# Two plain pairs and one pair ahead at the start of each projection, their results kept until the blocks are made

## The chip, the cores and the metric

The kernel runs on one core of one Trainium2 chip. The metric is the device time of one execution in microseconds (us). Its engines have queues of their own: TensorE (PE) multiplies, VectorE (DVE) and ScalarE (ACT) do elementwise work, GpSimd (POOL) issues transfers here, SyncE (SP) issues most transfers. PEld is TensorE's loading of weights.

## What is computed

Two layers of a hybrid encoder trunk over 1024 tokens of width 1024. Cut to what matters:

```python
for l in range(DEPTH):                      # DEPTH = 2
    h = rmsnorm(x, norm1_w[l])
    q, k, v, g, z, xbc, dt_raw, lru_gate, lru_x = split_proj(h @ w_in[l])
    y_ret = retention(q, k, v, g)
    y_ssd = ssd(z, xbc, dt_raw, ...)
    y_lru = rglru(lru_gate, lru_x, ...)
    y = jnp.concatenate([y_ret, y_ssd, y_lru], axis=-1)
    x = x + (y @ w_out[l]).astype(x.dtype)
    h = rmsnorm(x, norm2_w[l])
    x = x + conv_ffn(h, ffn_w_up[l], ffn_conv_w[l], ffn_conv_b[l], ffn_w_down[l])
return rmsnorm(x, final_norm_w)
```

`conv_ffn` multiplies by `ffn_w_up`, runs a causal convolution of width 3 over the tokens, gates one half with the other and multiplies by `ffn_w_down` (2816 wide). The ssd part runs a convolution of width 4 over x, B and C, and takes its step sizes dt from eight columns of the projection through a softplus; their running sums (cum) make the decays.

## The kernel before

**Products.** Everything is float32. A number is split into a high part of type fp32r and a low rest, and each product takes three passes: high times high, high times low, low times high. The high part of a weight is a ScalarE copy (L236), the low part a VectorE subtraction (L243) or, in the steady state (`by_dma`), a second ScalarE copy and a transfer that POOL issues and that subtracts on the way (L241). An operand's low part is L206. A `product` here is 12 matmuls of 128x512: four slices of the contraction, three passes each.

**Four projections.** Each layer has two: the input projection (12 pairs of 128-column weight tiles, in an order written out by hand) and the feed-forward up projection (22 pairs). Each pair meets the 1024 tokens in two halves of 512, and the width of 1024 in two halves, so a pair is a 2 by 2 block product. In the plain way that takes 8 products. By the Winograd form of Strassen's scheme it takes 7, with sums of weight tiles (`prep`, L710: named wr and s) and sums of operand blocks. The operand blocks have names: b11 and b21 are the first token half, made early from a normalised half (XA); t1, b22, t2, t3 and t4 need the second half (XB) and its norm too, and `blocks_b` makes them in this order: XB is scaled by its norm `rows` (L744, L746, L750), then differences (L710) and splits (L206).

**The opening of a projection.** `products` starts with `lead` pairs in the plain way and `ahead` pairs begun in the Winograd way, before the second half's norm and blocks are there. `lead` makes the first token half of a plain pair from b11 and b21 (4 products; the second of two added at L809), `follow` the second half from t1 and b22 (4 products, L822). `start` makes the first token half of a Winograd pair (2 products, L837), `end` the other 5, with t2, t3, t1, b22 and t4 in that order (L874 to L890). Between the leads `rest(j)` does the steps of the second half's norm and blocks. Before the change lead is 1 and ahead 2 everywhere:

```python
        n = lead + ahead
        for j, p in enumerate(pairs[:n]):
            if j < lead:
                p.lead(raw)
            else:
                p.start(True, raw)
            if j < n - 1:
                rest(j)
        rest(2)
```

**What is done with a result.** Each finished tile goes to the pair's `take` at once: in the feed-forward part the convolution (`conv`: a ScalarE step L315 and VectorE steps L318, tile fc) and the gate (L933); in the input projection a rotation for q and k (L382 to L384, tiles c, u, qs, tb), a convolution for x, B and C (L318 and L393, tile xb), gelu, silu or the LRU's gates. In layer 0 the first leads run on unnormalised input and are multiplied by the norm `raw` afterwards (L847, L848).

**dt and cum.** `steps` multiplies dt's 16 columns (L403, 16 matmuls for one half of the tokens, tile dt, summed to dtc at L407 to L415), transposes the result on TensorE (L418, bank dtt), and adds the bias (L421, L422). `ssd_dt` runs the softplus on VectorE in small steps (L173 to L182), multiplies to da, makes running sums with two small matmuls (L506, L507, tile cum), and transposes the sums (L519). Each engine has its own list of instructions, in the order in which the program was built.

## Time and profile before

| | |
|---|---|
| median of three runs | 2349.01 us (2347.21 to 2349.03) |
| the profiled execution | 2346.2 us |
| its span | 2344.4 us |
| PE, DVE, ACT busy share of the span | 93%, 82%, 55% |
| granted TensorE clock, mean | 0.97 of full speed |

The span is the time from the first to the last instruction of the profiled execution; 1.8 us lie around it. An engine is busy while it works on an instruction; what it waits for is shown by the idle time ahead of an instruction and by what released it. In a timeline an operation's duration is longer than the time to the next one's start, since neighbours overlap by some 0.08 us.

### The profile page before, as it was taken

The numbers are of one execution on the slowest core, as the hardware profiler recorded it, in microseconds if no ns is written. First come the engines' busy times: TensorE is split into PE (matmuls) and PEld (weight loads), VectorE is DVE, ScalarE is ACT, GpSimd is POOL, SyncE is SP. The second block draws the span as 40 slices with busy tenths as digits, with TensorE's granted clock in tenths as the row PEclk, the third lists the DMA queues.
The fourth block names the chain that finished last, engine by engine and source line by source line (L and its number), as shares of the span: only waits on it lengthen the run. The fifth ranks groups of instructions, "written<-read, shape, count | busy, mean of one in ns | idle before, by whom it ended". The sixth has DMA issues, their size and how long they took to land.

```text
span 2344.4 us, 31562 instructions
## 1 busy us (share of the span) xinstructions
PE 2174.7 (93%) x10494; PEld 1758.3 (75%) x10494; DVE 1924.6 (82%) x3763; ACT 1288.4 (55%) x2370; POOL 302.6 (13%) x335
## 2 busy tenths in 40 slices
PE   6699988997999999999978989899989999999997
PEld 4477767885788888878866767777668888887787
DVE  7987858779877788999798877696797788789987
ACT  5357637554566556444445674674556665654443
POOL 0012213000222222000001131210002222210000
PEclk9799999999999999999988999999989999999999
DMA  4365687561666666854334638846437666677522
GB/s 173 108 149 134 150 248 233 167 209 48 149 150 148 145 153 152 285 193 137 108 128 123 152 79 235 266 150 208 137 93 164 144 148 148 147 197 254 178 83 73
DMA packets 176147, 371.94 MB, mean 159 GB/s; under 512 B 19440, under 2 KB 31856, under 8 KB 175984
## 3 DMA queue, kind: packets, MB, share of 16 engines
q1 hardware_dynamic: 135760, 297.55, 38.6%
q0 software_dynamic: 37440, 68.17, 17.1%
q10 hardware_dynamic: 2784, 4.20, 0.5%
q8 instruction: 83, 1.36, 0.3%
q14 instruction: 80, 0.66, 0.1%
HBM read 228.22 MB, written 69.27 MB: 127 GB/s over the span
## 4 chain that ended last, share of the span: by engine, by line
PE 65%; DVE 15%; DMA 8%; issue 7%; ACT 3%; SPq 1%; POOL 1%; DVEq 0%; POOLq 0%; ACTq 0%
PE up L300 43%; PE op L300 6%; PE dy L995 5%; PE dx L995 5%; PE dx L1071 2%; DMA ws<-wr 2%; DVE ws L243 2%; DVE bl L206 1%; DVE xb L318 1%; DMA cumb<-cumscr 1%; DMA tb<-in_rope_dram 1%; DMA g<-g1scr 1%; DMA g<-g0scr 1%; DVE g L710 1%; DMA wr<-in_w_ct_dram 1%
## 5 line engine op out<-in xcount | busy, mean ns | idle before, releaser
L300 PE MATMUL up<-bh,ws 128*128 128x512 f32 x3840 | 1228.2, 400 | 76.4 <-ACT ws L236 50.5
L300 PEld LDWEIGHTS up<-bh,ws 128*128 128x128 f32 x3840 | 735.6, 192 | 249.7 <-ACT ws L236 54.0
L300 PE MATMUL up<-bl,ws 128*128 128x512 f32 x1920 | 761.1, 398 | 11.8 <-DVE bl L206 11.7
L236 ACT ACTIVATE ws<-wr 128x512 fp32r<-128x512 f32 x568 | 348.7, 626 | 358.9 <-PE up L300 129.0
L300 PEld LDWEIGHTS up<-bl,ws 128*128 128x128 f32 x1920 | 369.2, 192 | 102.3 <-DVE bl L206 22.4
L241 POOL DMA_DIRECT2D ws<-wr x222 | 197.6, 905 | 1321.5 <-ACT ws L240 1046.0
L243 DVE TENSOR_TENSOR ws<-wr,ws 128x512 fp32r<-128x512 f32 x346 | 236.5, 688 | 61.0 <-ACT ws L236 54.9
L995 PE MATMUL dy<-ws,ws 128*128 128x512 f32 x792 | 192.2, 390 | 3.2 <-ACT ws L236 1.6
L995 PE MATMUL dx<-ws,ws 128*128 128x512 f32 x792 | 190.8, 390 | 2.1 <-ACT ws L236 1.2
L995 PEld LDWEIGHTS dy<-ws,ws 128*128 128x128 f32 x792 | 148.2, 188 | 36.4 <-DVE ws L243 3.3
L995 PEld LDWEIGHTS dx<-ws,ws 128*128 128x128 f32 x792 | 148.4, 188 | 34.1 <-ACT ws L236 2.1
L318 DVE SCALAR_TENSOR_TENSOR fc<-u,smalls,fc 128x512 f32<-128x512 f32 (+2 forms) x176 | 131.0, 748 | 50.6 <-ACT fc L315 49.6
L240 ACT ACTIVATE ws<-ws 128x512 fp32r<-128x512 f32 x260 | 159.8, 626 | 4.6
L300 PE MATMUL op<-yh,ws 128*128 128x512 f32 x512 | 160.5, 394 | 0.2 <-ACT yh L213 0.2
L318 DVE SCALAR_TENSOR_TENSOR fc<-c,smalls,fc 128x512 f32<-128x512 f32 (+2 forms) x176 | 131.2, 745 | 0.7 <-ACT fc L315 0.3
L315 ACT ACTIVATE fc<-c,smalls 128x512 f32<-128x512 f32 x88 | 71.2, 809 | 103.7 <-DVE c L837 101.7
L243 DVE TENSOR_TENSOR ws<-g,ws 128x512 fp32r<-128x512 f32 (+1 forms) x165 | 103.1, 649 | 13.7 <-ACT ws L236 13.5
L236 ACT ACTIVATE ws<-g 128x512 fp32r<-128x512 f32 (+1 forms) x165 | 92.1, 590 | 39.7 <-PE dy L995 13.8
L300 PEld LDWEIGHTS op<-yh,ws 128*128 128x128 f32 x512 | 95.4, 188 | 21.7 <-ACT yh L213 2.1
L300 PE MATMUL op<-yl,ws 128*128 128x512 f32 x256 | 100.3, 394 | 0.0
L710 DVE TENSOR_TENSOR wr<-wr,wr 128x512 f32<-128x512 f32 x64 | 44.9, 702 | 63.0 <-DMA wr<-in_w_up_dram 28.3
L236 ACT ACTIVATE ws<-s 128x512 fp32r<-128x512 f32 x64 | 40.4, 632 | 101.3 <-DVE s L710 92.4
(303 smaller groups left out, 2939.3 us busy)
## 6 DMA issues: line engine op xcount, KB each, us to landing
ws<-wr POOLq DMA_DIRECT2D x222, 256.0 KB, 4.3
wr<-in_w_up_dram SPq DMA_DIRECT2D x96, 512.0 KB, 4.3
wr<-in_w_dn_dram SPq DMA_DIRECT2D x66, 512.0 KB, 3.9
wr<-in_w_ct_dram SPq DMA_DIRECT2D x56, 512.0 KB, 4.7
wr<-in_w_o_dram SPq DMA_DIRECT2D x32, 512.0 KB, 5.1
g0scr<-fc SPq DMA_DIRECT2D x44, 256.0 KB, 3.3
g<-g0scr SPq DMA_DIRECT2D x44, 256.0 KB, 5.8
g1scr<-fc SPq DMA_DIRECT2D x44, 256.0 KB, 2.9
```

What stands on the lines that cost most here:

```text
L206: eng.tensor_tensor(lo, src, hi.bitcast(F32), op=ALU.subtract)
L236: act.activation(w[:, 0, :m], raw, AF.Copy)
L240: act.activation(w[:, 1, :m], w[:, 0, :m].bitcast(F32), AF.Copy, scale=-1.0)
L241: pool.dma_start(w[:, 1, :m].bitcast(F32), raw, accum_op=ALU.add)
L243: eng.tensor_tensor(w[:, 1, :m], raw, w[:, 0, :m].bitcast(F32), op=ALU.subtract)
L300: pe.matmul(dst, W(k, a), A(k, b), start=first and i == 0, stop=last and i == n - 1)
L315: act.activation(dst, body(x), AF.Identity, bias=bias, scale=taps(n))
L318: dve.scalar_tensor_tensor(dst[:, o:HT], x[:, HALO - j + o : HALO - j + HT], taps(n - j), dst[:, o:HT], op0=ALU.mult, op1=ALU.add)
L710: eng.tensor_tensor(o, a, b, op=op)
L995: pe.matmul(d[oc], w[:, a, P * oc : P * oc + P], t[:, b], start=not more and i == 0 and k == 0, stop=i == NP - 1 and k == 2, skip_group_ch ...
L1071: pe.matmul(X[oc][:, e], w[x][:, P * oc : P * oc + P], t[:, y, e], start=False, stop=i == NP - 1 and k == 2, skip_group_check=True)
```

## The change

`products` begins with two pairs in the plain way and one in the Winograd way, in both layers and both kinds of projection. The takes of these three pairs are not called when a tile is done: `products` first runs `follow` of both plain pairs, `prep` of the pair ahead and all of `blocks_b`, then goes through the pairs and calls `firsts` (the takes of the first token half) and `followed` or `end`. t2 comes from another pool of tiles. The transposes of dt, the cum matmuls and the transposes of cum are held back by a count of products: `behind(n, f)` calls f when n more products have been issued, `tick` counts; cum's transposes get a bank of their own (cumt).

```diff
@@ -413,13 +416,17 @@
             dve.tensor_add(c, c, c1)
         else:
             dve.tensor_add(c, c1, d[0:16, :])
-        t = s_bank("dtt")
-        for i in range(4):
-            pe.transpose(t[:, 16 * i : 16 * i + 16], c[:, P * i : P * i + P], ident[0:16, 0:16])
         dt = s_tile("dt", [P, 4, 8], "dt")
-        t = t[:, 0:64].rearrange("p (c h) -> p c h", c=4)
-        dve.tensor_tensor(dt, t[:, :, 0:8], srow[:, l, 0, :].unsqueeze(1).to_broadcast([P, 4, 8]), op=ALU.add)
-        dve.tensor_add(dt, dt, t[:, :, 8:16])
+
+        def turn():
+            t = s_bank("dtt")
+            for i in range(4):
+                pe.transpose(t[:, 16 * i : 16 * i + 16], c[:, P * i : P * i + P], ident[0:16, 0:16])
+            t = t[:, 0:64].rearrange("p (c h) -> p c h", c=4)
+            dve.tensor_tensor(dt, t[:, :, 0:8], srow[:, l, 0, :].unsqueeze(1).to_broadcast([P, 4, 8]), op=ALU.add)
+            dve.tensor_add(dt, dt, t[:, :, 8:16])
+
+        behind(4, turn)
         return dt
 
     sret = {}
@@ -501,26 +508,34 @@
         softplus_of(e, dt, d, shp, "d")
         da = s_tile("da", shp, "da")
         dve.tensor_tensor(da, d, anea[:, l, :].unsqueeze(1).to_broadcast(shp), op=ALU.mult)
-        cps = s_bank("cum")
-        daf = da.rearrange("p c h -> p (c h)")
-        pe.matmul(cps[:, 0:32], tri, daf, start=True, stop=True)
-        pe.matmul(cps[:, 32:64], ones, daf, start=True, stop=True)
         cum = s_tile("cm", shp, "cm")
         ecum = s_tile("ec", shp, "ec")
         dec = s_tile("dc", shp, "dc")
         cdec = s_tile("cd", shp, "cd")
-        v = cps[:, 0:32].rearrange("p (c h) -> p c h", c=4)
-        last = cps[:, 32:64].rearrange("p (c h) -> p c h", c=4)
-        dve.tensor_copy(cum, v)
-        act.activation(ecum, cum, AF.Exp)
-        act.activation(cdec, last, AF.Exp)
-        dve.tensor_tensor(dec, last, cum, op=ALU.subtract)
-        act.activation(dec, dec, AF.Exp)
-        pe.transpose(cps[0:32, 128:256], cum.rearrange("p c h -> p (c h)"), ident)
-        ct = s_tile("ct", [32, P], "ct", 1)
-        act.activation(ct, cps[0:32, 128:256], AF.Copy)
-        sp.dma_start(scr[2 * l + h], ct)
-        dve.tensor_mul(dec, dec, d)
+
+        def sums():
+            cps = s_bank("cum")
+            daf = da.rearrange("p c h -> p (c h)")
+            pe.matmul(cps[:, 0:32], tri, daf, start=True, stop=True)
+            pe.matmul(cps[:, 32:64], ones, daf, start=True, stop=True)
+            v = cps[:, 0:32].rearrange("p (c h) -> p c h", c=4)
+            last = cps[:, 32:64].rearrange("p (c h) -> p c h", c=4)
+            dve.tensor_copy(cum, v)
+            act.activation(ecum, cum, AF.Exp)
+            act.activation(cdec, last, AF.Exp)
+            dve.tensor_tensor(dec, last, cum, op=ALU.subtract)
+            act.activation(dec, dec, AF.Exp)
+            dve.tensor_mul(dec, dec, d)
+            behind(3, turn)
+
+        def turn():
+            c = s_bank("cumt")
+            pe.transpose(c[0:32, 0:P], cum.rearrange("p c h -> p (c h)"), ident)
+            ct = s_tile("ct", [32, P], "ct", 1)
+            act.activation(ct, c[0:32, 0:P], AF.Copy)
+            sp.dma_start(scr[2 * l + h], ct)
+
+        behind(4, sums)
         return d, cum, ecum, dec, cdec
 
     def skip(l):
@@ -759,7 +774,7 @@
             put("b22", k, XB[4 + k], d_tile, d_tile)
         yield
         for k in range(4):
-            t = c_tile("t2")
+            t = t_tile("t2")
             sub(dve, t, XB[4 + k], XA[k])
             put("t2", k, t, aq_tile, aq_tile)
             scale_a(4 + k)
@@ -781,8 +796,22 @@
         sp.dma_start(r[:, : 2 * HT], src)
         return r[:, :HT], r[:, HT : 2 * HT]
 
-    def prod(d, w, B, name, first=True, last=True):
-        mm3(d, lambda k, a: w[:, a, P * k : P * k + P], lambda k, b: B[name, k][b], range(4), first, last)
+
+    pending = []
+
+    def behind(n, f):
+        pending.append([n, f])
+
+    def tick(n=1):
+        for x in list(pending):
+            x[0] -= n
+            if x[0] <= 0:
+                pending.remove(x)
+                x[1]()
+
+    def prod(d, w, B, name, first=True, last=True, more=False):
+        tick()
+        mm3(d, lambda k, a: w[:, a, P * k : P * k + P], lambda k, b: B[name, k][b], range(4), first and not more, last, more)
 
     class Pair:
@@ -790,7 +819,7 @@
         def __init__(self, src, B, take):
             self.src, self.B, self.take, self.ready, self.w, self.q = src, B, take, None, None, None
 
-        def lead(self, raw):
+        def lead(self):
 
             B = self.B
             self.v = []
@@ -808,8 +837,6 @@
                 c = halo(t_tile, "c11")
                 dve.tensor_add(body(c), body(u), d2)
                 self.v.append((c, u))
-                if not raw:
-                    self.take(m, 0, c, u)
 
         def follow(self):
@@ -820,14 +847,14 @@
                 prod(d, w1, self.B, "t1", last=False)
                 prod(d, w2, self.B, "b22", first=False)
                 dve.tensor_add(body(u), body(u), d)
+
+        def followed(self):
+            for m, (_, u) in enumerate(self.v):
                 self.take(m, 1, u)
 
-        def start(self, reload=False, raw=False):
-            if self.ready:
-                w11, w12 = self.ready
-            else:
-                q = up_raw(self.src[0])
-                w11, w12 = part_of(q[0]), part_of(q[1])
+        def start(self, reload=False):
+            q = up_raw(self.src[0])
+            w11, w12 = part_of(q[0]), part_of(q[1])
             d1, d2 = p_bank("up"), s_bank("up")
             prod(d1, w11, self.B, "b11")
             self.u = halo(c_tile, "u")
@@ -837,15 +864,17 @@
             dve.tensor_add(body(c11), body(self.u), d2)
             self.q = None if reload else q
             self.v = [(c11, self.u)]
-            if not (reload and raw):
-                self.scaled()
 
         def scaled(self):
 
-            for m, (c, u) in enumerate(self.v):
-                if "raw" in self.B:
+            if "raw" in self.B:
+                for c, u in self.v:
                     dve.tensor_tensor(body(c), body(c), self.B["raw"], op=ALU.mult)
                     dve.tensor_tensor(body(u), body(u), self.B["raw"], op=ALU.mult)
+
+        def firsts(self):
+
+            for m, (c, u) in enumerate(self.v):
                 self.take(m, 0, c, u)
 
         def prep(self):
@@ -892,31 +921,33 @@
             self.take(1, 1, C22)
 
 
-    def products(pairs, rest, later, lead, ahead, raw=False):
+    def products(pairs, rest, later, lead=2, ahead=1):
+
 
         n = lead + ahead
         for j, p in enumerate(pairs[:n]):
             if j < lead:
-                p.lead(raw)
+                p.lead()
             else:
-                p.start(True, raw)
-            if j < n - 1:
-                rest(j)
-        rest(2)
+                p.start(True)
+            rest(j)
+        for p in pairs[:lead]:
+            p.scaled()
+            p.follow()
+        pairs[lead].prep()
+        rest(3)
         for j, p in enumerate(pairs):
             by_dma[0] = j >= n
             if j >= n:
                 p.start()
-            elif raw:
+            if j >= lead:
                 p.scaled()
-            if j == 1:
-                rest(3)
-            if j < lead:
-                p.follow()
-            else:
-                p.end()
+            p.firsts()
+            (p.followed if j < lead else p.end)()
             for f in later.get(j, ()):
                 f()
+        while pending:
+            tick()
         by_dma[0] = False
 
     def ffn_pair(l, j, B):
@@ -1233,7 +1264,7 @@
             rest = lead(B, XA, XB, first[0])
             pairs[0].ready = ready
         later = {0: [] if l else [setup], 1: [dt_a, dt_b], 3: [dt_c]}
-        products(pairs, rest, later, *((1, 2) if l else (1, 2)), not l)
+        products(pairs, rest, later)
         after = mixers(l, dts, skip(l))
         XA = out_proj(l, 0, y_split(l, 0, after), src)
         SB = y_split(l, 1, last_dma[0])
@@ -1250,7 +1281,7 @@
         XB = out_proj(l, 1, SB, src, hook)
         sB = squares(lambda k: XB[k], f=d_tile)
         spill(xs1, XB, 1)
-        products([ffn_pair(l, j, B) for j in range(NF)], rest_of(B, XA, XB, sB, w2), {}, *((1, 2) if l else (1, 2)))
+        products([ffn_pair(l, j, B) for j in range(NF)], rest_of(B, XA, XB, sB, w2), {})
         XA, XB, last, others = ffn_down(l, None)
         if l + 1 < DEPTH:
             B, st = {}, {}
```

Two further hunks give `mm3` a flag that is never set and split `lru` into two functions with the same steps in the same order. Line numbers move: L809 becomes L838, L822 L849, L837 L864, L874 to L890 become L903 to L919, L710 L725, L744 L759, L933 L964, L382 to L384 become L385 to L387, L393 L396, L418 L424.

**Where instructions move.** First, VectorE in layer 0's feed-forward projection, ahead of the first Winograd pair that is not started early. Before, the sum s of the second pair ahead (s_5505) stands behind the end of the first one and among its convolution steps (fc):

```order
L886 TENSOR_TENSOR u_5123<-u_5123,up_5454 128x512
L890 TENSOR_TENSOR u_5436<-u_5436,up_5473 128x512
L710 TENSOR_TENSOR wr_5500<-wr_5500,wr_5502 128x512
L318 SCALAR_TENSOR_TENSOR fc_5468<-u_5123,smalls,fc_5468 128x512
L318 SCALAR_TENSOR_TENSOR fc_5487<-u_5436,smalls,fc_5487 128x511
L318 SCALAR_TENSOR_TENSOR fc_5468<-u_5123,smalls,fc_5468 128x512
L318 SCALAR_TENSOR_TENSOR fc_5487<-u_5436,smalls,fc_5487 128x510
L320 COPY c_5437<-u_5436 128x2
L710 TENSOR_TENSOR s_5505<-wr_5502,wr_5500 128x512
L933 TENSOR_TENSOR fc_5487<-fc_5139,fc_5487 128x512
L318 SCALAR_TENSOR_TENSOR fc_5494<-c_5437,smalls,fc_5494 128x512
L243 TENSOR_TENSOR ws_5507<-s_5505,ws_5507 128x512
```

After, the steps of all first pairs stand together ahead of the next pair's low weight part (ws_5643), and the end of the pair ahead and the sum s_5685 of the next pair follow:

```order
L318 SCALAR_TENSOR_TENSOR fc_5540<-c_5220,smalls,fc_5540 128x510
L964 TENSOR_TENSOR fc_5534<-fc_5529,fc_5534 128x512
L320 COPY u_5206<-c_5220 128x2
L903 TENSOR_TENSOR u_5206<-u_5206,up_5546 128x512
L243 TENSOR_TENSOR ws_5643<-wr_5637,ws_5643 128x512
L908 TENSOR_TENSOR u_5573<-u_5206,up_5560 128x512
L725 TENSOR_TENSOR wr_5637<-wr_5637,wr_5682 128x512
L911 TENSOR_TENSOR u_5206<-u_5206,up_5576 128x512
L912 TENSOR_TENSOR c_5574<-u_5573,up_5576 128x512
L915 TENSOR_TENSOR u_5206<-u_5206,up_5591 128x512
L919 TENSOR_TENSOR u_5573<-u_5573,up_5610 128x512
L725 TENSOR_TENSOR s_5685<-wr_5682,wr_5637 128x512
```

What moved: the steps L318 of the leads, which stood between the leads, now lie ahead of this place, and the sum s is that of pair 3 instead of pair 2.

Second, VectorE in layer 1's input projection, where the first pair ahead gets its weight sums (wr, s; here _11008 to _11015). Before, they stand at the end of the blocks, of which bl_10984 and those after it are the low parts, and of the rotations (qs_10931, u_10647):

```order
L206 TENSOR_TENSOR bl_10984<-xd_8698,bh_10983 128x512
L383 TENSOR_TENSOR qs_10931<-qs_10931,tb_10937 128x512
L206 TENSOR_TENSOR bl_10989<-xd_8700,bh_10988 128x512
L384 TENSOR_TENSOR u_10647<-u_10647,qs_10931 128x512
L206 TENSOR_TENSOR bl_10993<-xd_9756,bh_10992 128x512
L710 TENSOR_TENSOR wr_11008<-wr_11008,wr_11010 128x512
L206 TENSOR_TENSOR bl_10997<-xd_9758,bh_10996 128x512
L710 TENSOR_TENSOR s_11013<-wr_11010,wr_11008 128x512
L206 TENSOR_TENSOR bl_11001<-xd_9760,bh_11000 128x512
L710 TENSOR_TENSOR wr_11010<-wr_11010 128x512
L206 TENSOR_TENSOR bl_11005<-xd_9762,bh_11004 128x512
L243 TENSOR_TENSOR ws_11015<-s_11013,ws_11015 128x512
```

After, they come right behind the last low part of b22 and the first results of `follow` (L849), ahead of the difference t2 (t_11032):

```order
L206 TENSOR_TENSOR bl_10869<-xd_10293,bh_10868 128x512
L243 TENSOR_TENSOR ws_10979<-wr_10974,ws_10979 128x512
L725 TENSOR_TENSOR wr_11008<-wr_11008,wr_11010 128x512
L849 TENSOR_TENSOR u_10619<-u_10619,up_10880 128x512
L725 TENSOR_TENSOR s_11013<-wr_11010,wr_11008 128x512
L725 TENSOR_TENSOR wr_11010<-wr_11010 128x512
L849 TENSOR_TENSOR u_10657<-u_10657,up_10914 128x512
L243 TENSOR_TENSOR ws_11015<-s_11013,ws_11015 128x512
L243 TENSOR_TENSOR ws_11018<-wr_11008,ws_11018 128x512
L243 TENSOR_TENSOR ws_11022<-wr_11010,ws_11022 128x512
L725 TENSOR_TENSOR wr_11008<-wr_11008,s_11013 128x512
L725 TENSOR_TENSOR t_11032<-xd_10287,xd_9771 128x512
```

What moved: the sums, from behind the blocks t2 to t4 and two rotations to ahead of them.

Third, TensorE in layer 0's input projection at the dt transposes. Before, the first one stands behind a product of the first pair ahead (up_911), with dt's second product behind it:

```order
L300 MATMUL up_911<-bh_816,ws_841 128x512
L300 MATMUL up_911<-bl_817,ws_841 128x512
L300 MATMUL up_911<-bh_816,ws_841 128x512
L418 MATMUL dtt_965<-mats,dtc_962 128x16 x4
L403 MATMUL dt_973<-bh_514,wds 16x512
L403 MATMUL dt_973<-bl_515,wds 16x512
L403 MATMUL dt_973<-bh_521,wds 16x512
```

After, both stand behind pair 3's product by t1 (up_1231), and a product of the pair ahead by b22 (up_1072) follows:

```order
L300 MATMUL up_1231<-bh_566,ws_1189 128x512
L300 MATMUL up_1231<-bh_573,ws_1189 128x512
L300 MATMUL up_1231<-bl_574,ws_1189 128x512
L300 MATMUL up_1231<-bh_573,ws_1189 128x512
L424 MATMUL dtt_1073<-mats,dtc_997 128x16 x4
L424 MATMUL dtt_1080<-mats,dtc_1018 128x16 x4
L300 MATMUL up_1072<-bh_578,ws_759 128x512
L300 MATMUL up_1072<-bl_579,ws_759 128x512
L300 MATMUL up_1072<-bh_578,ws_759 128x512
```

What moved: the first transposes, past the end of the pair ahead and into pair 3, and the dt products to ahead of them.

## Rows read from the trace of the kernel before

**Rows 1.** The profile page's head: span, and busy time of each engine.

```profile
span 2344.4 us, 31562 instructions
...
PE 2174.7 (93%) x10494; PEld 1758.3 (75%) x10494; DVE 1924.6 (82%) x3763; ACT 1288.4 (55%) x2370; POOL 302.6 (13%) x335
```

**Rows 2.** By stage: length; busy PE, PEld, DVE, ACT, POOL (count); clock, DMA, GB/s.

```profile
23.00:130.00 107.00, 77.55 (x297) 51.59 (x298) 99.16 (x216) 38.94 (x76) 2.26 (x3) 0.84 0.30 95
520.00:588.00 68.00, 53.44 (x218) 38.93 (x216) 59.60 (x114) 33.16 (x53) 0.00 (x0) 0.92 0.18 54
588.00:962.00 374.00, 374.00 (x1637) 309.08 (x1638) 302.08 (x504) 223.67 (x363) 75.94 (x88) 0.99 0.65 156
1190.00:1290.00 100.00, 78.11 (x333) 58.39 (x333) 87.47 (x183) 44.66 (x77) 6.04 (x7) 0.86 0.43 129
1660.00:1733.00 73.00, 58.68 (x235) 43.11 (x233) 62.07 (x117) 35.80 (x56) 0.00 (x0) 0.91 0.17 58
```

**Rows 3.** The chain of waits (start us, us, engine, tile, line, count).

```profile
518.83 10.88 PE up L300 x48
...
587.94 373.61 PE up L300 x1635
...
1265.74 3.81 PE dt L403 x16
...
1732.38 373.17 PE up L300 x1635
```

**Rows 4.** Timeline of PE, layer 0's feed-forward opening (in brackets: idle before, releaser).

```profile
587.94 0.79 PE L300 MATMUL up<-bh,ws 128*128 128x512 f32 x1 [5.42 <-ACT ws L236]
```

**Rows 5.** Timeline of DVE there (start us, us, line, operation, count).

```profile
572.03 1.88 DVE L710 TENSOR_TENSOR xr<-xr,xr 128x512 f32<-128x512 f32 x3
...
583.16 0.68 DVE L710 TENSOR_TENSOR wr<-wr,wr 128x512 f32<-128x512 f32 x1
...
583.76 2.73 DVE L318 SCALAR_TENSOR_TENSOR fc<-u,smalls,fc 128x512 f32<-128x512 f32 x4
...
586.48 0.68 DVE L710 TENSOR_TENSOR s<-wr,wr 128x512 f32<-128x512 f32 x1
```

**Rows 6.** Timeline of PE, layer 0's input projection.

```profile
109.28 0.60 PE L418 MATMUL dtt<-mats,dtc 16*128 16x16 f32 x4 [10.02 <-DVE dtc L413]
...
114.79 0.40 PE L300 MATMUL up<-bh,ws 128*128 128x512 f32 x1
...
159.25 0.28 PE L519 MATMUL cum<-mats,cm 128*32 128x128 f32 x1 [4.00 <-DVE dc L517]
```

**Rows 7.** Timeline of DVE there.

```profile
47.17 2.08 DVE L750 SCALAR_TENSOR_TENSOR x<-x,first,nr 128x512 f32<-128x512 f32 x3 [0.75 <-ACT nr L1163]
...
100.79 4.05 DVE L318 SCALAR_TENSOR_TENSOR xb<-u,smalls,xb 128x512 f32<-128x512 f32 x6
...
108.55 0.67 DVE L413 TENSOR_TENSOR dtc<-dtc,dtc 16x512 f32<-16x512 f32 x1
```

**Rows 8.** Timeline of PE, layer 1's input projection.

```profile
1240.40 0.80 PE L300 MATMUL up<-bh,ws 128*128 128x512 f32 x1 [17.09 <-ACT ws L236]
```

**Rows 9.** Timeline of DVE there.

```profile
1201.14 0.69 DVE L744 TENSOR_TENSOR xd<-xd,rows 128x512 f32<-128x512 f32 x1 [2.08 <-ACT rows L736]
...
1239.00 0.68 DVE L710 TENSOR_TENSOR s<-wr,wr 128x512 f32<-128x512 f32 x1
```

**Rows 10.** The page's DMA issues: KB each, median us from issue to landing.

```profile
ws<-wr POOLq DMA_DIRECT2D x222, 256.0 KB, 4.3
wr<-in_w_up_dram SPq DMA_DIRECT2D x96, 512.0 KB, 4.3
```

**Rows 11.** Busy time in two stretches around that wait (PEclk: third from last).

```profile
1230.00:1240.00 10.00, 0.00 (x0) 0.00 (x0) 10.00 (x18) 4.47 (x8) 0.00 (x0) 0.50 0.30 105
1240.00:1250.00 10.00, 9.60 (x31) 7.51 (x32) 7.12 (x12) 2.65 (x5) 0.00 (x0) 0.71 0.30 105
```

More of the change, by code (lines that the diff above doesn't have):

```diff
@@ L299, in mm3 @@
             for a, b in PASSES:
-                pe.matmul(dst, W(k, a), A(k, b), start=first and i == 0, stop=last and i == n - 1)
+                pe.matmul(dst, W(k, a), A(k, b), start=first and i == 0, stop=last and i == n - 1, skip_group_check=more)
                 i += 1
```

4 lines of the change are left out of this document (3 added, 1 removed).

## Prediction

> **What bounds the kernel now.** I read the page's head first. TensorE (PE) is busy 93% of the span, VectorE (DVE) 82% [rows 1]. That looks like a TensorE kernel, but the shares are averages over stages, so the second view was the busy time by stage [rows 2]. There the reader is to see two regimes. From 588 to 962 us TensorE is busy for the whole window: inside a feed-forward projection nothing but the number of matmuls counts. In the four openings it is not: TensorE is busy 77.55 of 107 us in 23 to 130, 53.44 of 68 in 520 to 588, 78.11 of 100 in 1190 to 1290 and 58.68 of 73 in 1660 to 1733. That leaves 29.5 + 14.6 + 21.9 + 14.3 = 80 us of idle TensorE, while VectorE is busy 99 of 107, 60 of 68, 87 of 100 and 62 of 73 us. The openings are VectorE's.
>
> Third, the chain of waits [rows 3]: four products (48 matmuls) take 10.88 us, so a product of 12 matmuls takes 2.72. From 587.94 one unbroken piece of TensorE runs 373.61 us to the end of the feed-forward projection; 155 - 17 = 138 products stand there, 2.71 us each. Layer 1 repeats it from 1732.38, 373.17 us. So a feed-forward projection ends when its last opening stall ends, plus 2.71 us for each product then left. That is my tool for all four: how late is the last opening stall, and how many products are left behind it.
>
> **What the last stalls are.** In the feed-forward opening TensorE waits 5.42 us until 587.94 for a weight [rows 4]. On VectorE the weight's sum stands behind the pair's convolution steps: wr at 583.16, four steps, then s at 586.48 [rows 5]. In layer 0's input projection the last is 10.02 us at the dt transposes, until 109.28; at 114.79 the two dt products are done, 17 of 85 products are behind and 68 ahead; a further 4.00 us goes at the cum transpose [rows 6]. VectorE makes six conv steps just ahead of the dtc that is waited for [rows 7]. In layer 1's it is one wait of 17.09 us until 1240.40, with 12 of 85 products made and 73 ahead [rows 8]: the weight's sum s comes only at 1239.00, behind 38 us of block scaling, block differences and rotations since 1201.14 [rows 9].
>
> **The change, part by part.** *Two plain pairs and one ahead in place of one and two.* A plain pair costs 8 products, a pair made ahead 7. Each projection gets one product more, 12 matmuls or 2.72 us; four of them are 48 matmuls, 10.9 us of TensorE if no idle time covers them. In exchange 4 + 4 + 2 = 10 products (27.2 us) can run before the first t1 or b22 block is wanted, where 4 + 2 + 2 = 8 (21.8 us) could, and 8 more then need only t1 and b22 instead of 4. VectorE drops 6 instructions of 0.60 us in each projection (12 in a plain pair for 18), 3.6 us. Each opening also reloads one weight pair of 512 KB more; the queues move little then, so I cost it at nothing. If that cover were gone it costs a landing, 4.3 us [rows 10], once in a projection.
>
> *Results wait for the blocks.* No work goes away, only its place. In VectorE's list of the feed-forward opening the convolution steps of the first pairs leave the gaps between the leads and stand together ahead of the first weights of pair 3. So the 5.42 us wait goes, and pair 3's weights are late instead. Priced by the list: from c_5137's add to the sum s_5685 stand 99 VectorE instructions. With 0.60 us for a 512-column operation (three take 1.88) and 0.66 for a step of a convolution (four take 2.73) [rows 5] they sum to 58.4 us. c_5137 is the sixth product of the projection that begins at 518.83, so it is added at about 535.2; with some 4 us of waits for TensorE s_5685 is done at 597.7. Then its two parts: ScalarE behind the convolutions' first steps (1 to 3 us), the low part by POOL's transfer (4.3 from issue to landing [rows 10], and an issue): 603 to 606. TensorE is at pair 3's third product by then, having made 25 of 156 and waited 9 to 16 us, with 131 left. 604.5 + 131 x 2.71 + 0.9 (matmuls right after the stall at the lower clock) = 960.4, against 961.55 now. **Feed-forward: -1.2 us each, from +2.5 to -5**; layer 1 repeats layer 0's list.
>
> *The input projection of layer 1.* The preparation of the ahead pair's weights now stands on VectorE before the t2 to t4 blocks and the rotations, so the 17.09 us wait should go. What is late next is the dt transposes: they now stand behind pair 3's product by t1. From the first scaled block to the second dtc VectorE has 97 instructions, 58.5 us by the same prices; it starts 2 us later than the 1201.14 of now (one more product pair ahead of the norm), and waits some 3.7 us for products: 1265.4. Then 26 of 86 products are made and 60 left, with both dt products (16 matmuls each, 3.81 us for one [rows 3]) behind. Now, from 1240.40, 73 products and 7.5 us of dt are left: 1240.4 + 198.6 + 7.5 = 1446.5. After: 1265.4 + 163.2 = 1428.6, plus a new wait of some 7 us where the cum matmuls stand behind the softplus chain, plus 2.5 us of lower clock: 1438. The clock is in the rows: after the 17 us without a matmul the granted clock is 0.50 (1.2 GHz), and 0.71 over the ten us that follow [rows 11]. **-8 us.**
>
> *The input projection of layer 0.* Blocks start 2 us later than 47.17 [rows 7], since two more products lie ahead of the norm's transposes: 49.2. From there to the dtc stand 118 VectorE instructions, 71.7 us: 120.9. Then 60 of 86 products are left, 163.2 us, and some 9 us of waits at the two cum matmuls: 293. Now: 114.79 + 68 x 2.72 + 4.0 = 303.8. That is 10.7; the tail of this projection waits for transfers and conv results that I leave as they are, so I take **-9**.
>
> Deferring transposes by counted products, t2 from another pool, the cum transpose's own bank: I cost these at nothing beyond the waits above; what covers them is that the first readers of dt and cum come products later. Buffers held longer could add a wait at a copy into u: between nothing and one rotation's write-out, some 4 us.
>
> **Sum.** The profiled execution took 2346.2 us; -9 - 8 - 1.2 - 1.2 = -19.4 gives 2326.8. The median of the runs shown is 2349.01, 2.8 above the profiled one: 2329.6, so **2329.5 us** (-0.8%).
>
> **Rivals.**
> 1. *The backlog only moves.* VectorE's list is as long as before but for 3.6 us a projection, so the new waits (pair 3's weights, dtt, cum) eat what the old ones gave. For it: VectorE is busy over 85% in all openings. Against it: at the new stall more products are behind. It gives 2344 to 2353.
> 2. *Slower: the extra product is paid in full.* A feed-forward projection loses as soon as pair 3's weights land after 605.2 us, less than 1 us behind my own estimate, and each us later is lost one for one; the input projections lose when the dtc comes after 1273 and 131 us. With weights some 4 us later, for instance behind ScalarE's convolution steps, and the input projections no better, the time is 2349 + 10.9 = 2360. [...]
> 3. *Full cover.* VectorE gets ahead, and most of the 80 us of idle TensorE goes, less 10.9: half of it gives 2320, all 2280. Against it: VectorE's own 58 to 72 us between blocks and dtc stand in the way.
>
> **How the numbers follow.** About 0.2% (4.7 us) is what a measurement of this kernel can tell from no change. Forecast (2315 to 2340): 0.5. Rival 3: 0.17, below 2315. Rival 1: 0.18, of which 0.03 ends below 2344. Rival 2: 0.15. So faster 0.70, within 0.2% 0.15, slower 0.15. The range leaves out half of rival 3 and most of rival 2: 2304 to 2354; the forecast's own range is 2315 to 2340.
>
> **What would show it.** Right: in the feed-forward openings the wait before the ahead pair's second weight is gone and one of 9 to 16 us stands before pair 3's third product near 604 and near 1749; the unbroken TensorE piece behind it is about 355 us. In layer 1's input projection no wait of 17 us, but one at the dt transposes ending near 1265, and one at cum of some 7 us. The granted clock in 1230 to 1240 is above 0.5. Wrong: a stall of pair 3 that ends after 607 (the feed-forward term turns), a dtt wait that ends after 1273, a copy into u that waits for a rotated tile's write-out, or a tail behind 130 us that swallows what layer 0's opening gained.

## The result, and the profile after

The change made the kernel slower: 2366.81 us (median of 4, 2362.74 to 2367.53) against 2348.32 of the kernel before; the ratio is 1.0076 [1.0058, 1.0093]. Forecast were 2329.5 us, and the time is above the upper end of the range too. Run again, the changed kernel took 2365.7 against 2347.51, ratio 1.007 [1.0055, 1.0084]. The profiled execution of after took 2362.74 us.

The head of its page, which answers to [rows 1]:

```profile
span 2360.9 us, 31654 instructions
...
PE 2187.3 (93%) x10542; PEld 1777.9 (75%) x10542; DVE 1916.5 (81%) x3739; ACT 1293.0 (55%) x2380; POOL 305.7 (13%) x337
```

The 48 matmuls more are there (10494 to 10542), the VectorE instructions less too (3763 to 3739). TensorE's busy time grew by 12.6 us and the span by 16.5: the extra products were paid, and 4 us of idle time on top.

Busy time by stage, columns as in [rows 2], for the four openings:

```profile
23.00:130.00 107.00, 83.42 (x339) 59.82 (x339) 99.01 (x207) 44.08 (x84) 5.32 (x6) 0.86 0.42 121
530.00:620.00 90.00, 77.00 (x333) 61.41 (x332) 78.11 (x143) 46.76 (x76) 2.59 (x3) 0.92 0.27 82
1190.00:1290.00 100.00, 88.23 (x386) 68.23 (x385) 86.49 (x159) 50.78 (x88) 5.19 (x6) 0.93 0.47 140
1683.00:1780.00 97.00, 83.61 (x355) 65.91 (x354) 80.09 (x147) 50.04 (x81) 5.18 (x6) 0.91 0.32 90
```

The openings did fill: 339 matmuls where 297 stood in 23 to 130, and 386 where 333 stood in 1190 to 1290 (that opening begins 8.8 us later now, so it is a looser reading). So the loss lies behind the openings, or in stages that the prediction did not look at. The chain of waits, where the feed-forward projections answer to [rows 3]:

```profile
530.56 10.88 PE up L300 x48
...
647.06 324.00 PE up L300 x1429
...
1778.30 351.63 PE up L300 x1539
```

I cut the program into stages to find the rest. A projection runs from its first to its last matmul into a tile `up`; what follows, up to the next projection, is the mixers with the output projection, or the down projection with what follows it. P1 and P2 are the input projections of layers 0 and 1, M1 and M2 the mixers behind them, F1 and F2 the feed-forward stages with their down projections. From the timelines of TensorE, in us (differences taken before rounding):

| stage | before | after | difference | forecast |
|---|---|---|---|---|
| P1 | 334.1 | 342.6 | +8.5 | -9 |
| M1 | 176.6 | 180.2 | +3.5 | 0 |
| F1 | 662.3 | 659.4 | -2.9 | -1.2 |
| P2 | 304.6 | 309.1 | +4.4 | -8 |
| M2 | 176.6 | 184.0 | +7.4 | 0 |
| F2 | 674.8 | 670.9 | -3.9 | -1.2 |
| sum | | | +17.0 | -19.4 |

The feed-forward terms have the right sign. Both input projections became slower instead of faster, and so did both mixers, which the diff doesn't touch.

**What stands in the openings now.** TensorE's timeline of after, the waits that answer to [rows 4, 6, 8]:

```profile
124.77 1.03 PE L424 MATMUL dtt<-mats,dtc 16*128 16x16 f32 x8 [10.83 <-DVE dtc L416]
...
155.21 0.41 PE L519 MATMUL cum<-da,mats 128*128 128x32 f32 x2 [4.67 <-DVE da L510]
...
240.65 0.65 PE L300 MATMUL up<-bh,ws 128*128 128x512 f32 x1 [2.75 <-ACT u L861]
...
284.79 0.79 PE L300 MATMUL up<-bh,ws 128*128 128x512 f32 x1 [5.19 <-ACT ws L236]
...
606.48 1.22 PE L300 MATMUL up<-bh,ws 128*128 128x512 f32 x2 [8.19 <-DVE ws L243]
...
612.25 0.50 PE L300 MATMUL up<-bh,ws 128*128 128x512 f32 x1 [1.83 <-ACT ws L236]
...
616.89 1.22 PE L300 MATMUL up<-bh,ws 128*128 128x512 f32 x2 [2.98 <-DMA ws<-s]
...
1268.66 0.79 PE L300 MATMUL up<-bh,ws 128*128 128x512 f32 x1 [4.00 <-ACT u L861]
...
1279.63 0.58 PE L424 MATMUL dtt<-mats,dtc 16*128 16x16 f32 x4 [6.58 <-DVE dtc L418]
1281.40 0.61 PE L424 MATMUL dtt<-mats,dtc 16*128 16x16 f32 x4 [1.19 <-DVE dtc L418]
...
1310.07 0.80 PE L300 MATMUL up<-bh,ws 128*128 128x512 f32 x1 [4.49 <-ACT ws L236]
```

The waits of 5.42 us [rows 4] and 17.09 us [rows 8] are gone. In F1 three waits of together 13.0 us stand before pair 3's products (forecast: 9 to 16 us). F1 begins 11.73 us later than before (530.56 for 518.83), so the last of them, until 616.89, ends at 605.2 on the scale of before, where the forecast had 604.5. The dt wait of P1 ends at 124.77 (forecast 120.9). P2 has two, one for each token half, and the second ends 1281.40 - 1189.76 = 91.6 us after that projection begins, where the forecast had 1265.4 - 1181.14 = 84.3. And two rows, 240.65 and 284.79, stand 116 and 160 us behind the dt transposes, in a stretch where I had assumed that nothing changes.

### The profile page after: what moved, and what is told of

Its sections match the earlier page's. It is cut to its first block, busy times and chain, and to the rows that moved or that the text cites. A ratio compares the mean times of both kernels' runs of the same rounds, so it can differ in the third digit from the quotient of the medians.

```text
span 2360.9 us, 31654 instructions
## 1 busy us (share of the span) xinstructions
PE 2187.3 (93%) x10542; PEld 1777.9 (75%) x10542; DVE 1916.5 (81%) x3739; ACT 1293.0 (55%) x2380; POOL 305.7 (13%) x337
## 4 chain that ended last, share of the span: by engine, by line
PE 62%; DVE 19%; DMA 9%; issue 5%; ACT 3%; SPq 1%; POOL 1%; DVEq 0%; ACTq 0%; POOLq 0%
PE up L300 39%; PE op L300 6%; PE dy L1026 6%; PE dx L1026 6%; DMA ws<-wr 2%; PE dx L1102 2%; DVE ws L243 2%; DVE xb L318 2%; DMA tb<-in_rope_dram 2%; DVE fc L318 1%; DVE bl L206 1%; DMA cumb<-cumscr 1%; DVE wr L725 1%; DMA wr<-in_w_ct_dram 1%; DMA g<-g0scr 1%
## 5 line engine op out<-in xcount | busy, mean ns | idle before, releaser
L300 PEld LDWEIGHTS up<-bh,ws 128*128 128x128 f32 x3872 | 744.6, 193 | 270.0 <-ACT ws L236 59.6
L236 ACT ACTIVATE ws<-wr 128x512 fp32r<-128x512 f32 x576 | 354.1, 625 | 356.3 <-PE up L300 121.4
L300 PEld LDWEIGHTS up<-bl,ws 128*128 128x128 f32 x1936 | 374.0, 193 | 85.5 <-DVE bl L206 4.7
L318 DVE SCALAR_TENSOR_TENSOR fc<-u,smalls,fc 128x512 f32<-128x512 f32 (+2 forms) x176 | 130.9, 748 | 46.4 <-ACT fc L315 45.4
L318 DVE SCALAR_TENSOR_TENSOR fc<-c,smalls,fc 128x512 f32<-128x512 f32 (+2 forms) x176 | 130.5, 745 | 0.4 <-ACT fc L315 0.4
L315 ACT ACTIVATE fc<-u,smalls 128x512 f32<-128x512 f32 x88 | 70.9, 807 | 35.8 <-DVE u L915 32.1
```

What stands on the lines that cost most here:

```text
L236: act.activation(w[:, 0, :m], raw, AF.Copy)
L300: pe.matmul(dst, W(k, a), A(k, b), start=first and i == 0, stop=last and i == n - 1, skip_group_check=more)
L315: act.activation(dst, body(x), AF.Identity, bias=bias, scale=taps(n))
L318: dve.scalar_tensor_tensor(dst[:, o:HT], x[:, HALO - j + o : HALO - j + HT], taps(n - j), dst[:, o:HT], op0=ALU.mult, op1=ALU.add)
```

## The experiments

Theory H: holding the results costs, since VectorE and ScalarE get the held work in one piece, in front of what TensorE needs next. Theory P: two plain pairs cost, because their extra product is paid in full. Later came theory S: what counts is the order into which the whole program is put when it is built, the mixers of layer 1 above all.

Every kernel below is the changed kernel with a switch for each projection: how many plain pairs, how many ahead, whether results are held (if not, taken as before the change), whether dt and cum are counted (deferred behind counted products; if not, as before), and the pool of t2. With the values of before everywhere the program has the instructions of before, row for row. As the changed kernel, in the notation of the diffs below (layer 0, layer 1):

```python
IN = ((2, 1, True, True, 't'), (2, 1, True, True, 't'))
FF = ((2, 1, True, True, 't'), (2, 1, True, True, 't'))
```

All results in one table; stages in us from one profiled execution each, times and ratios from 5 rounds beside the kernel before on the same chip:

| kernel | us | before | ratio | P1 | M1 | F1 | P2 | M2 | F2 |
|---|---|---|---|---|---|---|---|---|---|
| e1_ffn_only | 2343.2 | 2349.17 | 0.9977 [0.9967, 0.9987] | 336.5 | 177.3 | 659.5 | 305.1 | 178.5 | 669.0 |
| e2_in_only | 2356.98 | 2349.17 | 1.004 [1.0026, 1.0053] | 343.7 | 177.7 | 660.7 | 301.4 | 186.0 | 673.9 |
| e3_in_2and1_at_once | 2350.92 | 2349.17 | 1.0007 [0.9998, 1.0015] | 340.7 | 178.5 | 662.4 | 296.2 | 184.9 | 673.7 |
| e4_in_1and2_held | 2351.64 | 2349.17 | 1.0014 [1.0001, 1.0027] | 340.0 | 179.6 | 660.8 | 297.6 | 184.4 | 674.7 |
| a_again | 2365.7 | 2347.51 | 1.007 [1.0055, 1.0084] | 343.3 | 179.7 | 659.2 | 313.0 | 184.6 | 670.5 |
| e5_in_held_no_count | 2353.97 | 2347.51 | 1.0025 [1.0015, 1.0034] | 339.8 | 180.7 | 659.8 | 301.1 | 184.7 | 672.7 |
| e6_in_count_only | 2360.54 | 2347.51 | 1.0053 [1.0034, 1.0071] | 334.9 | 177.4 | 662.5 | 309.8 | 184.9 | 673.9 |
| e7_in_2and1_count | 2344.5 | 2347.51 | 0.9984 [0.9972, 0.9996] | 336.1 | 178.1 | 660.6 | 295.7 | 183.7 | 675.1 |
| e8_not_held_old_mixers | 2341.3 | 2348.82 | 0.9966 [0.9951, 0.9981] | 336.8 | 180.4 | 659.3 | 300.8 | 176.9 | 671.7 |
| e9_p2_as_before_new_mixers | 2341.54 | 2348.82 | 0.9968 [0.9956, 0.9981] | 335.0 | 178.3 | 659.5 | 296.3 | 184.2 | 670.6 |
| e10_p2_changed_third_order | 2347.08 | 2348.82 | 0.9994 [0.9982, 1.0006] | 336.8 | 177.1 | 661.8 | 302.6 | 179.1 | 671.2 |
| e11_change_not_held | 2351.65 | 2348.82 | 1.0008 [0.9997, 1.0019] | 333.9 | 179.1 | 658.9 | 306.2 | 185.1 | 671.1 |

How finely a stage can be read: the two profiles of the changed kernel differ by under 1 us in five stages and by 3.9 in P2, and P1 as before (e1, e10) reads 336.5 and 336.8 where before has 334.1. A difference of 3 or 4 us in one stage says little.

**e1_ffn_only and e2_in_only: one part alone.**

```diff
-IN = ((2, 1, True, True, 't'), (2, 1, True, True, 't'))
+IN = ((1, 2, False, False, 'c'), (1, 2, False, False, 'c'))
```

> The change in the two feed-forward projections alone; both input projections as before. By the traces of before and after, the stretches with a feed-forward projection are 2.9 and 4.1 us shorter after the change and those with an input projection 11.7 and 11.8 us longer. If the stretches are independent (theory A), this kernel takes 2348.3 - 7 = 2341 us, faster than before. Rival B: the extra product is paid in full wherever it is made, and the feed-forward stretches look shorter only because of what came ahead of them; then 2348.3 + 5.4 = 2354 us.

```diff
-FF = ((2, 1, True, True, 't'), (2, 1, True, True, 't'))
+FF = ((1, 2, False, False, 'c'), (1, 2, False, False, 'c'))
```

> The change in the two input projections alone; both feed-forward projections as before. Theory A (independent stretches): 2348.3 + 23.5 = 2372 us, and the dt transposes wait until near 125 us in layer 0. Rival B (a product more costs 2.7 us everywhere and the rest is spread): about 2360 us.

The feed-forward half gains 0.23%, 5.4 us of 2349; the other half loses 0.4%, 9.4 us. So the change is two changes of different sign, and its loss comes with the input projections: in e2 it stands in P1 (+9.5) and in the mixers behind P2 (M2 +9.4), while P2 gains 3.2.

**e3_in_2and1_at_once and e4_in_1and2_held: the two halves of the loss.** The pairs alone, with results, dt and cum taken as before; then the holding together with the counting, with the pairs as before.

```diff
-IN = ((2, 1, True, True, 't'), (2, 1, True, True, 't'))
+IN = ((2, 1, False, False, 't'), (2, 1, False, False, 't'))
```

> Input projections with two plain pairs and one ahead, but each result is taken at once as before, and the dt and cum steps are not held back; feed-forward as before. Theory H (holding the results back is what costs: the convolutions, rotations and gates come later, VectorE and ScalarE are behind in the tail): the loss of 23.5 us goes, 2345 to 2354 us. Rival P (the pair composition costs: a product more and the blocks wanted by four follow products more): most of it stays, 2362 to 2372 us.

```diff
-IN = ((2, 1, True, True, 't'), (2, 1, True, True, 't'))
+IN = ((1, 2, True, True, 't'), (1, 2, True, True, 't'))
```

> Input projections with one plain pair and two ahead as before, but the results wait for the blocks and the dt and cum steps are held back by products as in the change; feed-forward as before. Theory H (holding costs): 2362 to 2375 us. Rival P (the composition costs): 2345 to 2352 us.

Each costs some 0.1% or nothing, and together (e2) they cost 0.4%: neither theory holds alone. e3's time is in the range of theory H, e4's in that of theory P. The stages show why the sums hide it. In both, P2 gains 7 to 8 us, nearly what I had forecast for it, and M2 takes that back, 184 to 185 us for 176.6, though nothing in the mixers' code is different.

**a_again, e5_in_held_no_count, e6_in_count_only, e7_in_2and1_count.** The changed kernel once more, then the remaining parts of the input projections one by one (feed-forward as before).

```diff
-IN = ((2, 1, True, True, 't'), (2, 1, True, True, 't'))
+IN = ((2, 1, True, False, 't'), (2, 1, True, False, 't'))
```

```diff
-IN = ((2, 1, True, True, 't'), (2, 1, True, True, 't'))
+IN = ((1, 2, False, True, 'c'), (1, 2, False, True, 'c'))
```

```diff
-IN = ((2, 1, True, True, 't'), (2, 1, True, True, 't'))
+IN = ((2, 1, False, True, 't'), (2, 1, False, True, 't'))
```

> The changed kernel itself once more, on the same chip as the next three. The two halves of the change, measured apart, gave -6 us (feed-forward alone) and +9 us (input projections alone); if they add up (theory A), this takes before + 4 us, ratio 1.001 to 1.003. If the whole is more than its halves (theory C: a projection's opening depends on how the stage ahead of it ended), it takes before + 16 to 20 us as in its first runs, ratio 1.006 to 1.009.

> Input projections with two plain pairs and one ahead, results held until the blocks are made, but the dt and cum steps are not held back by counted products; feed-forward as before. Theory H (the held results cost): like the input projections' half of the change, before + 7 to 12 us. Rival D (the counting costs, since it puts the dt and cum transposes behind more products and their readers later): before - 3 to + 4 us.

> Input projections as before (one plain pair, two ahead, results taken at once), only the dt and cum steps held back by counted products; feed-forward as before. Theory H: before - 4 to + 2 us, since nothing waits for dt and cum for a while and the 10 us wait at dtt is moved behind other products. Rival D: before + 4 to 10 us.

> Input projections with two plain pairs and one ahead, results taken at once, dt and cum held back by counted products; feed-forward as before. Theory H (holding results costs): before to before + 4 us, like the same without the count (ratio 1.0007). Rival D (the count costs): before + 6 to 12 us.

The whole loses 16.4 us again where its halves add up to 4. e5, between the ranges of theory H and rival D, loses 5.9; e6 loses 12.4, more than either expected, and not in P1 but in P2 and M2; e7, expected at before or slower, is faster. Counting alone is the worst single part (1.0053), and together with two plain pairs it is the best (0.9984). The parts don't add up, so no theory that gives each part a price can be right. Without holding, P1 is at 336.1 (e7) where e2's, held, is at 343.7; and M2 is slow in all of e2 to e7.

**e8 to e11: the order of the mixers.** TensorE's list of M2 takes one of three orders in these kernels. Where layer 1's ssd products of one chunk begin, the list of before, then that of after (numbers in the names are counters):

```
L461 MATMUL rst_13309<-kv_13284 128x128 x2
L456 MATMUL ry_13297<-kv_13284,sT_13295 64x64 x8
L544 MATMUL cb_13353<-x_12948,x_12944 128x128
L550 MATMUL xsp_13358<-mats,x_12934 128x128
L550 MATMUL xsp_13358<-mats,x_12936 128x128
```

```
L468 MATMUL rst_13343<-kv_13318 128x128 x2
L463 MATMUL ry_13331<-kv_13318,sT_13329 64x64 x8
L559 MATMUL cb_13387<-x_12980,x_12976 128x128
L559 MATMUL cb_13387<-x_12982,x_12978 128x128
L565 MATMUL xsp_13392<-mats,x_12968 128x128
```

In the first the first half of `cb` stood 29 rows ahead, in the second both halves stand here; the `gtr` and `zp` matmuls, the gates of the chunk before, now stand among `xsp`. The source of these lines is the same. I chose four kernels by their lists: e8 has M2 in the order of before behind a changed P2; e9 has P2's source as before and M2 in the order of after; e10 has the whole change in P2 alone and M2 in the third order; e11 is the change without holding in the input projections, M2 as after.

```diff
-IN = ((2, 1, True, True, 't'), (2, 1, True, True, 't'))
+IN = ((2, 1, False, True, 't'), (2, 1, False, False, 't'))
```

```diff
-IN = ((2, 1, True, True, 't'), (2, 1, True, True, 't'))
+IN = ((2, 1, False, True, 't'), (1, 2, False, False, 'c'))
```

```diff
-IN = ((2, 1, True, True, 't'), (2, 1, True, True, 't'))
-FF = ((2, 1, True, True, 't'), (2, 1, True, True, 't'))
+IN = ((1, 2, False, False, 'c'), (2, 1, True, True, 't'))
+FF = ((1, 2, False, False, 'c'), (1, 2, False, False, 'c'))
```

```diff
-IN = ((2, 1, True, True, 't'), (2, 1, True, True, 't'))
+IN = ((2, 1, False, True, 't'), (2, 1, False, True, 't'))
```

> Feed-forward as in the change. Input projections with two plain pairs and one ahead but results taken at once; dt and cum counted in layer 0, not counted in layer 1. This mix is chosen because the program then lists layer 1's mixers on TensorE row for row as before the change. Theory S (two things cost: the results held back in the input projections, some 6 us each, and another order of layer 1's mixers, which no line of the change touches, 7.5 us): P1 336, P2 296, mixers of layer 1 177 us, in all before - 14, 2334 us. Rival R (whatever is done to an input projection, the mixers behind it grow as the projection shrinks): mixers 184 us, 2342 us.

> Layer 1's input projection is written as before the change; layer 0's has two plain pairs and one ahead with results taken at once and counted dt and cum; feed-forward as in the change. The program lists layer 1's mixers in the changed order all the same. Theory S: mixers of layer 1 184 to 186 us, P2 305, in all about before + 2, 2350 us. Rival R: mixers of layer 1 177 us, 2343 us.

> The whole change in layer 1's input projection alone, all else as before. The mixers behind it stand in a third order, that of the kernel with the feed-forward part alone (178.5 us there). Theory S: mixers of layer 1 177 to 179 us although the projection is fully changed, P2 301 to 310; in all before - 3 to + 6. Rival R: mixers 184 to 186 us, before + 4 to + 13.

> The change with one thing undone: in the input projections results are taken at once instead of waiting for the blocks (the counting of dt and cum, two plain pairs and one ahead, and all of the feed-forward part stay). Layer 1's mixers stand in the changed order. Theory S: P1 336, P2 296, mixers 184, feed-forward parts 7 shorter, in all before - 6, 2342 us. Rival C (the whole of the change is more than its parts whether or not results are held): 2355 us or more.

Busy time by stage in P2 (first row) and in M2 (second), for e8:

```profile
1184.78:1485.59 300.81, 265.55 (x1119) 206.17 (x1118) 237.88 (x429) 166.23 (x290) 46.95 (x50) 0.94 0.59 158
1485.59:1662.50 176.91, 166.89 (x1234) 140.62 (x1234) 142.06 (x431) 110.51 (x279) 24.94 (x22) 0.99 0.65 210
```

The same for e9:

```profile
1180.76:1477.07 296.31, 259.47 (x1107) 203.37 (x1106) 240.57 (x435) 167.37 (x288) 47.52 (x50) 0.94 0.59 158
1477.07:1661.29 184.22, 169.15 (x1235) 140.49 (x1234) 149.00 (x431) 111.32 (x278) 25.83 (x22) 0.99 0.62 202
```

And for after:

```profile
1189.76:1498.82 309.06, 269.90 (x1119) 210.67 (x1118) 235.78 (x429) 167.19 (x290) 46.96 (x50) 0.92 0.57 154
1498.82:1682.80 183.98, 168.26 (x1234) 140.81 (x1234) 148.96 (x431) 111.25 (x278) 25.80 (x22) 0.99 0.62 202
```

In these 14 profiles M2 goes with its order: 176.6 and 176.9 us in the order of before (before, e8), 178.5 and 179.1 in the third (e1, e10), 183.7 to 186.0 in that of after (the ten others), whether P2 ahead of it takes 295.7 or 313.0. TensorE has 1234 or 1235 matmuls in all three fences, VectorE 431 instructions, but VectorE is busy 149 us for them in e9 and after, 142 in e8.

The stage M2 came out as theory S says in all four, but the times of e8 and e9 did not: 2341.3 and 2341.54, where S expected 2334 and 2350. In e8 M1 (180.4) and P2 (300.8 for 296) were longer than S had them, and in e9 P2 took 296.3 for 305.

P2 may do the same. Its source as before takes 304.6 us (before), 305.1 (e1) and, listed otherwise behind a changed P1, 296.3 (e9, 1107 matmuls like before). The whole change in P2 takes 301.4 (e2) and 302.6 (e10), and 309.1 and 313.0 where the feed-forward part ahead of it is changed too. Two plain pairs, counted, not held take 295.7 (e7) and 306.2 (e11). These steps of 6 to 11 us are as large as anything that I had priced. e11's time came out some 10 us above what I expected of it, as much as its P2 did (306.2 for 296). But that P2's order causes these steps is not shown: each of these kernels has a list of its own in P2, so that the order can't be told apart from the stage ahead of it, and P2 of the changed kernel alone read 309.1 and 313.0. e7's and e11's P2 differ in 3 places of 1118 matmuls, and in 72 of 441 VectorE instructions.

## Why the prediction was wrong

What failed is the input projections' share of the sum, -9 and -8 forecast and +8.5 and +4.4 measured, and the mixers' share, which was put at nothing and measured +3.5 and +7.4. The tool behind the first was that a projection ends when its last opening stall ends, plus 2.7 us for each product left. The rows that it was read from are of the feed-forward projections, and there it held. In the input projections it does not hold: by it P1 of before ends at 303.8 us and P2 at 1446.5, and they end at 342.0 and 1485.6. The 38 and 39 us between were carried over as if the change didn't move them. TensorE's timeline of e7 shows that a stall in the opening doesn't settle the end:

```profile
1260.42 0.79 PE L300 MATMUL up<-bh,ws 128*128 128x512 f32 x1 [19.46 <-ACT ws L236]
```

Its P2 has this wait of 19.46 us and is 13.4 us shorter than that of after, where no wait of the opening is over 7 us.

**Feed-forward: right, with its size too small.** The 5.42 us wait went, pair 3's weights came late at the place and by the amount foreseen. Forecast -1.2 each; measured in the stages -2.9 and -3.9, and -5.4 us in e1's time, which is this half alone. The last stall ended 0.7 us later than forecast, with 25 products behind as I had it, and the piece of TensorE after it, from 616.89 to 971.06 (647.06 + 324.00), took 354.2 us for 355.9. That makes -2.2 at the end of the piece, 971.06 - 11.73 = 959.3 for 961.55; the rest is within the reading.

**Input projection of layer 0: two steps failed.** The first is "Blocks start 2 us later ... 120.9". They began at 47.66, earlier than forecast, but the dtc came 3.9 us later, the last of 10.83 us of waiting: the sum had no waits in it, and VectorE waited 4.6 us on the way, 2.5 of them for the rotation's tables. The transposes stood behind 25 products instead of 26. The second is the larger: "the tail of this projection waits for transfers and conv results that I leave as they are". The prediction names this tail among its signs of being wrong, and it came. In the stretch 230 to 300, 100 us behind the dt transposes, TensorE gets through 239 matmuls in after:

```profile
230.00:300.00 70.00, 60.30 (x239) 46.44 (x239) 52.03 (x85) 37.64 (x60) 13.73 (x14) 0.93 0.51 130
```

In e11, the same program with results not held in the input projections, it gets through 286:

```profile
23.00:130.00 107.00, 80.80 (x338) 59.06 (x338) 103.00 (x216) 43.88 (x86) 2.73 (x3) 0.87 0.35 110
230.00:300.00 70.00, 68.18 (x286) 53.96 (x285) 51.59 (x81) 38.73 (x65) 18.94 (x20) 0.98 0.71 172
```

In the opening the two are level, 339 and 338 matmuls, so holding gains nothing there, although the busy time of after is 2.6 us longer. ScalarE's timeline of after shows what stands ahead of the 5.19 us wait of the tail:

```profile
283.56 0.63 ACT L395 ACTIVATE c<-xb 128x512 f32<-128x512 f32 x1 [4.27 <-DVE xb L318]
284.11 1.23 ACT L236 ACTIVATE ws<-wr 128x512 fp32r<-128x512 f32 x2
```

The copy of the weight's high parts stands behind the silu of a result, and that waits for the result's last convolution step on VectorE. That looks like held work that came back, but two other runs say that it is not the holding. In e3 nothing is held, and the same two waits, on TensorE and on ScalarE, stand there with 6.46 and 4.28 us:

```profile
282.84 0.79 PE L300 MATMUL up<-bh,ws 128*128 128x512 f32 x1 [6.46 <-ACT ws L236]
```

```profile
281.61 0.63 ACT L395 ACTIVATE c<-xb 128x512 f32<-128x512 f32 x1 [4.28 <-DVE xb L318]
```

In e5 results are held, and TensorE waits nowhere for over 2.1 us between 230 and 300. The stretch in e3, then in e5:

```profile
230.00:300.00 70.00, 58.58 (x225) 44.52 (x224) 50.32 (x80) 38.49 (x61) 14.57 (x15) 0.90 0.49 123
230.00:300.00 70.00, 65.74 (x281) 51.99 (x280) 53.66 (x83) 43.09 (x72) 19.66 (x21) 1.00 0.68 163
```

TensorE's order of the last 427 matmuls of P1 is the same in e3 as in after, and that of the last 406 the same in e5 as in e11. So this tail, too, goes with the order in which the program lists it; what in the edit decides that order stays open. Between e11 and a_again, which differ in the source by the holding alone, P1 goes from 333.9 to 343.3 (+9.4) and the time from 2351.65 to 2365.7 (before beside them: 2348.82 and 2347.51). With dt and cum counted, holding goes with 5 to 9 us more in P1 (e6 to e4, e7 to e2, e11 to a_again); without counting it changes nothing there (340.7 in e3, 339.8 in e5). P1 gained nothing even without holding (336.1 in e7, 336.8 in e8, 335.0 in e9, 333.9 in e11, for 334.1 to 336.8 as before). So the 9 us of forecast gain, in which the extra product was already counted, were lost in waits; I can't divide them further.

**Input projection of layer 1: the dt wait, and the order.** "58.5 us by the same prices" left out transfers. VectorE's timeline of after, where the held rotations are made ahead of the dtc:

```profile
1260.77 0.69 DVE L386 TENSOR_TENSOR qs<-qs,tb 128x512 f32<-128x512 f32 x1 [1.62 <-DMA tb<-in_rope_dram]
...
1268.69 0.69 DVE L385 TENSOR_TENSOR u<-u,tb 128x512 f32<-128x512 f32 x1 [3.88 <-DMA tb<-in_rope_dram]
...
1270.45 0.69 DVE L386 TENSOR_TENSOR qs<-qs,tb 128x512 f32<-128x512 f32 x1 [1.06 <-DMA tb<-in_rope_dram]
```

Those are 6.6 us of waits for the rotation's tables, for which the sum had no term. The second dt wait ends 7.4 us later than forecast: the blocks begin 2.2 us later (at 1214.00), and from there it is 67.4 us for 62.2, the 3.7 us that I had allowed for waits included. The 4.00 us at 1268.66 are the copy into u that I had put down as a possibility and not in the sum. On ScalarE it waits for the write-out of a rotated tile:

```profile
1268.01 0.60 ACT L861 ACTIVATE u<-up 128x512 f32<-128x512 f32 x1 [3.98 <-DMA qscr<-u]
```

That made P2 with the change 301 to 303 in e2 and e10: -2 to -3 instead of -8. The remaining 7 to 11 us of after and a_again come where P2 stands behind the changed feed-forward part and is listed otherwise; which of the two makes them stays open.

**The mixers: a term that was missing.** I compared the order of instructions at the openings and took the stages behind as fixed. M2's order had changed with the program, which could be read before the run, and M2 costs 7.4 us more. M1's +3.5 I did not separate; M1 is at 177.1 to 180.7 in all experiments.

**The rivals.** Rival 2 came nearest, by half of its mechanism: in the input projections the extra product is paid and nothing comes back (TensorE's busy time grew by 12.6 us in all, the price of the four products being 10.9). Its other half did not come, since the feed-forward weights landed at the point of 605.2 us and not behind it. The time passed its 2360 by 7 us, about what the mixers of layer 1 lost, which was in none of the rivals.

**What stays open**: why the order of after is slower inside M2 (a part is in the last section), and what in the edit decides between the orders. Fastest of all kernels here are e8 and e9, 0.34% and 0.32% below the kernel before, though their intervals overlap with that of e1 (0.23%). They share the change in the feed-forward projections, and in layer 0's input projection two plain pairs with counted dt and cum and the results taken as before.

## What to carry to other kernels

An edit at one place can re-list a stage far behind it, so compare the order of the whole program before pricing the edit, and measure each half of an edit by itself: this one held a gain of 5.4 us and a loss of 9.4, and the two together lost over 16. A rule that is read from one stage, such as an end that follows the last stall, has to be tried on the other stages of the kernel before, whose ends are known. When a wait seems to come from what was put off, look for the same wait in a kernel that puts nothing off. Price the waits of the instructions that move, their transfers too, and not their durations alone.

## What the hardware showed that I had not expected

A VectorE instruction on 2 columns can take nearly seven times its usual time. In M2 a square root is refined in steps of 128x2 elements (L190 to L192). GpSimd's timeline of e9 has a product of 512 columns:

```profile
1490.91 1.09 POOL L634 TENSOR_TENSOR ss<-ss,cd 128x512 f32<-128x512 f32 x1 [3.66 <-DVE gtt L191]
```

and VectorE's at the same time:

```profile
1489.36 0.15 DVE L192 SCALAR_TENSOR_TENSOR gy<-gtt,gy 128x2 f32<-128x2 f32 x1
...
1491.02 1.00 DVE L192 SCALAR_TENSOR_TENSOR gy<-gtt,gy 128x2 f32<-128x2 f32 x1
```

The second begins 0.11 us after GpSimd's and ends with it, near 1492.0: 1.00 us for 0.15. By groups of instructions over M2 (busy us, mean ns of one), e8 and then e9:

```profile
L192 DVE SCALAR_TENSOR_TENSOR gy<-gtt,gy 128x2 f32<-128x2 f32 x24 | 4.9, 204 | 0.1
```

```profile
L192 DVE SCALAR_TENSOR_TENSOR gy<-gtt,gy 128x2 f32<-128x2 f32 x24 | 7.3, 306 | 0.1
```

In e9 8 of the 72 steps of L190 to L192 overlap with a GpSimd instruction and take 0.88 us on average, in before 4, at 0.54; no step without such an overlap takes over 0.17. All 72 together take 16.7 us in e9 and 12.4 in before. That is a part of VectorE's 7 us more in M2, and fits its order, in which the gates stand among other chunks' work. It doesn't settle why M2 is slower: in e10 8 steps overlap, at 0.77, 15.9 us in all, and its M2 is only 2.5 us longer than that of before.

The Trainium skill (page SBUF — State Buffer, section "SBUF: two separate sides") says that VectorE and GpSimd share a pair of ports as an exclusive lock, and that the loser "fully blocks", also where VectorE reads two inputs from SBUF against a GpSimd instruction that reads it. The trace agrees, with the 1.00 us above.
